# Hybrid decoder layer, prompt and one decode token: the channel parameters loaded by GpSimd's queue in two halves and turned in the gates' first step, two sums of gate rows on GpSimd, the decode gates' product in another bank

## The chip, the cores and the metric

The kernel runs on one core of a Trainium2 chip. The metric is the device time of one execution in microseconds (us). Before the change the median of three runs is 956.1 us (955.97 to 957.79).

## The reference

One decoder layer with two groups of heads is computed for a prompt of 1024 tokens and for one token each of 8 running sequences, all in float32. Cut to what matters here:

```python
hn = rmsnorm(x, g_norm)
u = hn @ w_in                       # 1024 -> 7 * 1024 + 4 + 4
xa, za, uq, uk, uv, uo, zb, ui, uf = jnp.split(u, SPLIT_IDX, axis=-1)
yA, hA, bufA = rglru_branch(xa, conv0, h0, conv_w, conv_b, w_rgate, b_rgate, w_igate, b_igate, lru_lambda)
...
ig = ui + b_mi                      # input gate, 4 heads
lf = jax.nn.log_sigmoid(uf + b_mf)  # forget gate, 4 heads
hB, C, n, m = mlstm_seq(q, k, v, ig, lf, C0, n0, m0)
yB = jax.nn.sigmoid(uo) * hB ; yB = headwise_rmsnorm(yB) * g_mhead
merged = jnp.concatenate([yA * jax.nn.silu(za), yB * jax.nn.silu(zb)], axis=-1)
x = x + merged @ w_out
```

`rglru_branch` needs parameters for each of its 1024 channels: `conv_w` (4 values), `conv_b`, `b_rgate`, `b_igate`, `lru_lambda`. `mlstm_seq` needs, for each token and head, sums and running maxima of the two gates over time, which come from `lf` and `ig`: 4 heads by 1024 tokens.

## The kernel before

**How the work is tiled.** TensorE multiplies a float32 pair as three products of parts (`mm3`, lines 62 to 66: high by high, high by low, low by high). The parts are made by `split` (lines 68 to 71): ScalarE casts the high part, VectorE subtracts it for the low part (`cb_hi`, `cb_lo` of the input; `wh`, `wl` of the weights). `w_in` is worked in 14 units (`UNITS`, line 44), each of two blocks of 256 columns, named by what they make: `v0v1` is unit 0, `x0y0` unit 1, `q0k0` unit 2.

**A unit.** From unit 1 on a unit is made by seven products in place of eight (a Strassen-like scheme; they come in the order P1, P2, P5, P6, P7, P3, P4, and "the third product" is P5). Each is 24 matmuls of 128x512 in two parts of 12, in a bank of PSUM with the tag `kv` (two banks; P1, P6, P7, P4) or `o` (three banks; P2, P5, P3). `evac` (line 300) takes a part out of its bank: ScalarE copies some (`s`, `c`), VectorE adds others (lines 316 and beside it), and `emit_out` (line 337) stores the result by GpSimd's queue (`stq`; `d_x`, `d_y`, `d_v` are the places in DRAM). Loads go by SyncE's queue (`ld`). `prep` (line 254) makes the weights' parts two products ahead, in a ring of six buffers (`ws`); at the third product it first calls `dec_unit`.

**Decode.** `dec_unit(u)` (line 227) multiplies the 8 decode tokens `hnd` by a unit's weights: eight matmuls of 32x512 (line 232) into the one bank with the tag `tr`, a copy `Z`, and later four transposes of it (line 240) into the same bank.

**The prelude** (lines 470 to 521). Nine tiles of x are fetched, scaled by the norm on VectorE, transposed (line 390) and split. Between them unit 0 is multiplied plainly (`plain`), 264 columns wide, since the 8 columns of the gates' weights `wg` go along; `gs` holds the prompt's gates as columns. After the loop the decode tokens' gates are multiplied (`pgd`, lines 512 to 514, in the `tr` bank), biased (`gd`, line 516), and stored to DRAM by SyncE's queue. Then `dec_unit(0)` and the loads of unit 1's weights (`load_raw`) follow.

**The gates** (`gates`, line 529) are a generator. Its steps stand in a list (`bg`), and in unit 1 two of them are popped after each part of a product, later one. In order:

- The 49 rows of parameters `par` (9 sources) are loaded by SyncE's queue; GpSimd fills `msk` and `stk`; `dgb`, the decode gates on all partitions, is loaded.
- Eight transposes (line 549) turn `par` to columns, which one VectorE copy puts into `PT` (line 550).
- A chain of small steps makes the log-sigmoid of the forget gates and of `lru_lambda` together (`gx`, lines 553 to 579).
- Transposes turn `lf` and `gs` to rows of 4x1024 (line 588), which are copied into `rows` (line 589). Two scans on VectorE run over time (lines 593 and 594).
- `al` (line 597) and `br` (line 600) are differences of such rows, `gsm` holds a few values for each chunk (lines 604 to 607).
- `stk` gathers four blocks of four rows: two sums on VectorE (lines 612 and 614), two copies on ScalarE.
- After five empty steps its eight transposes follow (line 622), and copies and exponentials of them (lines 624 to 627).

**What sets the order.** The kernel is written in one order of calls; a scheduler orders the instructions of each engine and places the waits. Each engine then works through its own list in order, and so does each queue of DMAs.

The functions that the diff touches, with the line numbers of the profile:

Of the kernel before, what the change touches and what calls it, by code (L numbers as in the profile page):

```python
# [9 lines left out]
F32 = mybir.dt.float32  # L10
# [3 lines left out]
ALU = mybir.AluOpType  # L14
# [3 lines left out]
P = 128  # L18
T = 1024
HT = 512  # L20
NB = 8
KC = 8
NH = 4
NCH = 8
L = 128
# [4 lines left out]
R_CW, R_CB, R_BR, R_BI, R_LAM, R_GM, R_H0, R_CONV, R_N0, R_END = 0, 4, 5, 6, 7, 8, 9, 17, 41, 49  # L30
# [19 lines left out]
def hymba_kernel(  # L50
# [28 lines left out]
    def ps(tag, shape):  # L79
        return psp.tile(shape, F32, tag=tag, name=f"ps_{tag}", bufs=NBUF.get(tag, 1))  # L80

    def const(shape, name, dt=F32):
        return cpool.tile(shape, dt, tag=name, name=name)
# [10 lines left out]
    def ws(shape, name, dt=F32R):  # L94

        return wsp.tile(shape, dt, tag="ws", name=name)

    def sg(shape, name, dt=F32):

        return stg.tile(shape, dt, tag="stg", name=name)  # L100
# [4 lines left out]
    def dconst(shape, name):  # L105

        return dpool.tile(shape, F32, tag=name, name=name)


    idF = const([P, P], "idF")  # L110
# [7 lines left out]
    PT = dconst([P, KC, R_END], "PT")  # L118
    bgate = const([P, 8], "bgate")
    m0b = dconst([P, NB, NH], "m0b")  # L120
# [33 lines left out]
    d_gd = dram.tile([NB, 8], F32, name="d_gd")  # L154
# [72 lines left out]
    def dec_unit(u):  # L227

        pz = ps("tr", [P, 512])
        for k in range(KC):  # L230
            g = k % 4
            TE.matmul(pz[32 * g:32 * g + 32, :], hnd[:, NB * k:NB * k + 32], raws[u, k // 4][:, k % 4, :], start=k < 4, stop=k >= 4,  # L232
                      skip_group_check=True)
        Z = sg([P, 512], "Z")
        A.copy(Z, pz)

        def turn():
            pt = ps("tr", [P, 4, P])
            for m in range(4):
                TE.transpose(pt[:, m, :], Z[:, m * P:(m + 1) * P], idF)  # L240
            for a, (kind, j) in enumerate(units[u]):
                src = pt[:, 2 * a:2 * a + 2].rearrange("p m (g b) -> p m b g", g=4)[:, :, 0:NB, :]
                V.tensor_reduce(dec_dst[kind](j), src, axis=mybir.AxisListType.X, op=ALU.add)
                if kind == "k":
                    V.tensor_scalar(dec_dst[kind](j), dec_dst[kind](j), 1.0 / 16.0, None, op0=ALU.mult)
        late.append(turn)
# [115 lines left out]
    fp = es_f.enter_context(tc.tile_pool(name="f_start", bufs=1))  # L362
# [85 lines left out]
    def plain(i):  # L448
# [10 lines left out]
        for w in range(2):  # L459
# [7 lines left out]
                V.tensor_tensor(gs[:, i, :], pt[:, 256:264], bgate, op=ALU.add)  # L467
            stq(d_v[w][i * P:(i + 1) * P, :], t)

    pw = ps("tr", [P, P])  # L470

    for _ in range(17):
# [36 lines left out]
            plain(i)  # L509
            x_combos(i)  # L510

    pgd = ps("tr", [32, 8])
    for k in range(KC):
        TE.matmul(pgd, hnd[:, NB * k:NB * k + 32], wg[:, k, :], start=k == 0, stop=k == KC - 1)
    gd = dconst([NB, 8], "gd")
    V.tensor_tensor(gd, pgd[0:NB], bgate[0:NB], op=ALU.add)
    ld(d_gd, gd)
    dec_unit(0)
    load_raw(1, 0)
    load_raw(1, 1)  # L520
# [4 lines left out]
    fp = es_f.enter_context(tc.tile_pool(name="f_gates", bufs=1, reuse_waits="tile"))  # L525
# [1 line left out]
    LOHI = slice(0, 64), slice(64, 128)  # L527

    def gates():

        par = ws([R_END, T], "par", F32)
        ld(par[R_CW:R_CW + 4, :], conv_w[0])
        for r, t in ((R_CB, conv_b), (R_BR, b_rgate), (R_BI, b_igate), (R_LAM, lru_lambda), (R_GM, g_mhead)):
            ld(par[r:r + 1, :], t)
        ld(par[R_H0:R_H0 + NB, :], st_h[0])
        ld(par[R_CONV:R_CONV + 24, :], st_conv[0].rearrange("b j w -> (b j) w"))
        ld(par[R_N0:R_N0 + NB, :], st_n[0].rearrange("b h k -> b (h k)"))
        ld(m0b, st_m[0].partition_broadcast(P))
        stk = fp.tile([P, T], F32, tag="stk", name="stk")
        msk = fp.tile([NH, T], F32, tag="msk", name="msk")  # L540
        G.memset(msk, 1.0)
        G.memset(msk.rearrange("p (c l) -> p c l", l=L)[:, :, 0:1], 0.0)
        G.memset(stk, 0.0)
        dgb = fp.tile([P, NB, 8], F32, tag="dgb", name="dgb")
        ld(dgb, d_gd.partition_broadcast(P))
        yield
        pt = ps("s", [P, KC, 64])
        for j in range(KC):
            TE.transpose(pt[:, j, 0:R_END], par[:, j * P:(j + 1) * P], idF[:R_END, :R_END])
        V.tensor_copy(PT, pt[:, :, 0:R_END])  # L550
        yield

        gx = fp.tile([P, 6, 72], F32, tag="gx", name="gx")
        fx, ab, lg, z, z2, p = (gx[:, n, :] for n in range(6))
# [37 lines left out]
        mr, br = rows1[:, 0, :], rows1[:, 1, :]  # L592
# [3 lines left out]
        al = lfr  # L596
# [4 lines left out]
        c3 = lambda t: t.rearrange("p (c l) -> p c l", l=L)  # L601
        sm = fp.tile([NH, 3, NCH], F32, tag="gsm", name="gsm")
        mpv, aL, csr = sm[:, 0], sm[:, 1], sm[:, 2]
# [5 lines left out]
        ld(d_cs, csr)  # L609
        ld(cs_b, d_cs.partition_broadcast(P))  # L610
        yield
        V.tensor_tensor(c3(stk[0:4]), c3(al), mpv.unsqueeze(2).to_broadcast([NH, NCH, L]), op=ALU.add)
        A.copy(stk[32:36], br)
        V.tensor_tensor(c3(stk[64:68]), c3(br), aL.unsqueeze(2).to_broadcast([NH, NCH, L]), op=ALU.add)
        A.mul(stk[96:100], mr, -1.0)
        for _ in range(5):
            yield
        for half in range(2):
# [4 lines left out]
            s = slice(half * 4, half * 4 + 4)  # L623
# [10 lines left out]
    bg, rgq, dcq = deque(), deque(), deque()  # L634
# [740 lines left out]
    def preps(n):  # L1375
        while state["prep"] < min(n, len(seq)):
            prep(*seq[state["prep"]])
            state["prep"] += 1

    gg = gates()  # L1380
    bg.extend([lambda: next(gg, None)] * 17 + [rd_open])
    last_u = len(units) - 1
    unit_of = {p: u for u, pair in enumerate(units) for p in pair}
    done_h = [max(unit_of[k, h] for k in "qkv") for h in range(NH)]
# [60 lines left out]
    for n in range(4, N):  # L1445
        c, h = n // 4, n % 4
# [90 lines left out]
```

## Time and profile before

| what | value |
|---|---|
| median of three runs | 956.1 us (955.97 to 957.79) |
| the profiled execution, its own time | 955.33 us |
| its span in the profile | 953.5 us |
| its mean granted TensorE clock | 0.995 |
| TensorE (PE) busy | 929.5 us, 97% |
| VectorE (DVE) busy | 713.0 us, 75% |
| ScalarE (ACT) busy | 584.7 us, 61% |
| GpSimd (POOL) busy | 146.2 us, 15% |

Times in the rows of a timeline are microseconds from the start of the span. A row gives the start, the duration, the engine, the line of the code, the operation, and what it writes and reads (`out<-in`, the program's names with the buffer numbers left out, so that `ps_s` is the bank with the tag `s`). In square brackets stands how long the engine was idle just before, and what ended that. A row of waits gives the sum, the count and the longest. SPq and POOLq are the queues of DMAs that SyncE and GpSimd issue.

### The profile page before, as it was taken

To read this page: it belongs to the slowest core of one execution; us is meant where nothing else is said; L and a number is where in the kernel's file an instruction comes from. 1 tells how busy PE (TensorE), PEld (TensorE's weight loads), DVE (VectorE), ACT (ScalarE), POOL (GpSimd) and SP (SyncE) were. 2 spreads that over 40 slices of the span, in tenths; PEclk is the share of its full clock that TensorE was granted. 3 is DMA by queue.
4 is the path that set the end of the run, shared out by engine and by line. 5 is a ranking of instruction groups with operands and counts; after the bars stand their busy time and mean duration, and the time that the engine had idled before them with its cause. 6 is when DMAs were issued, how large, how long until landed. Compare 5 with 4: busy or idle time off the path is not lost.

```text
span 953.5 us, 15405 instructions
## 1 busy us (share of the span) xinstructions
PE 929.5 (97%) x5370; PEld 763.6 (80%) x5370; DVE 713.0 (75%) x1482; ACT 584.7 (61%) x1046; POOL 146.2 (15%) x259
## 2 busy tenths in 40 slices
PE   7999999999999999999999999999999999999997
PEld 7887767777787987776789998876567888888886
DVE  5876798879798877988887867686566677676754
ACT  5664347778677757677677774465546466555532
POOL 1111112112212122111122221010200100000020
PEclk9999999999999999999999999999999999999999
DMA  5441447355745465445647362534863654564361
GB/s 185 148 128 40 136 119 266 109 183 194 259 142 206 156 206 171 166 155 171 223 153 244 122 219 84 161 111 146 297 213 95 204 162 119 162 179 143 111 110 51
DMA packets 131363, 153.71 MB, mean 161 GB/s; under 512 B 15798, under 2 KB 110038, under 8 KB 131278
## 3 DMA queue, kind: packets, MB, share of 16 engines
q1 hardware_dynamic: 113558, 96.86, 34.1%
q0 software_dynamic: 17728, 55.87, 16.2%
q8 instruction: 42, 0.69, 0.3%
q14 instruction: 35, 0.29, 0.1%
HBM read 101.11 MB, written 51.65 MB: 160 GB/s over the span
## 4 chain that ended last, share of the span: by engine, by line
PE 75%; DVE 9%; DMA 7%; issue 4%; ACT 3%; SPq 1%; POOL 0%; DVEq 0%; ACTq 0%; POOLq 0%
PE ps_o L64 12%; PE ps_o L66 12%; PE ps_o L65 12%; PE ps_kv L64 9%; PE ps_kv L66 9%; PE ps_kv L65 9%; DMA W<-d_alpha 3%; PE ps_tr L232 2%; PE ps_s L1087 1%; DVE wl L71 1%; PE ps_qp L914 1%; DMA x<-in_x_prompt_dram 1%; PE ps_tr L1223 1%; PE ps_s L747 1%; PE ps_qp L64 1%
## 5 line engine op out<-in xcount | busy, mean ns | idle before, releaser
L70 ACT CAST wh<-raw 128x1024 fp32r<-128x1024 f32 x91 | 95.6, 1051 | 58.5 <-PE ps_o L65 22.7
L71 DVE TENSOR_TENSOR wl<-raw,wh 128x1024 fp32r<-128x1024 f32 x91 | 111.2, 1222 | 26.8 <-ACT wh L70 16.3
L64 PE MATMUL ps_kv<-cb_hi,wh 128*128 128x512 f32 x320 | 128.1, 400 | 0.4 <-ACT s L313 0.4
L66 PE MATMUL ps_kv<-cb_hi,wl 128*128 128x512 f32 x320 | 125.7, 393 | 0.0
L65 PE MATMUL ps_kv<-cb_lo,wh 128*128 128x512 f32 x320 | 125.1, 391 | 0.0
L64 PE MATMUL ps_o<-cb_hi,wh 128*128 128x512 f32 x240 | 95.0, 396 | 0.0
L66 PE MATMUL ps_o<-cb_hi,wl 128*128 128x512 f32 x240 | 94.1, 392 | 0.0
L65 PE MATMUL ps_o<-cb_lo,wh 128*128 128x512 f32 x240 | 93.4, 389 | 0.0
L64 PEld LDWEIGHTS ps_kv<-cb_hi,wh 128*128 128x128 f32 x320 | 60.1, 188 | 23.5 <-issue 5.5
L66 PEld LDWEIGHTS ps_kv<-cb_hi,wl 128*128 128x128 f32 x320 | 60.1, 188 | 15.6 <-issue 2.5
L65 PEld LDWEIGHTS ps_kv<-cb_lo,wh 128*128 128x128 f32 x320 | 60.2, 188 | 12.6 <-issue 0.8
L64 PE MATMUL ps_kv<-wh,cb_hi 128*128 128x256 f32 x192 | 55.4, 288 | 0.0
L65 PE MATMUL ps_kv<-wl,cb_hi 128*128 128x256 f32 x192 | 54.3, 283 | 0.0
L66 PE MATMUL ps_kv<-wh,cb_lo 128*128 128x256 f32 x192 | 54.3, 283 | 0.0
L64 PE MATMUL ps_o<-wo,rh 128*128 128x512 f32 (+1 forms) x136 | 53.8, 396 | 0.0
L64 PEld LDWEIGHTS ps_o<-cb_hi,wh 128*128 128x128 f32 x240 | 45.1, 188 | 10.7 <-issue 1.8
L66 PEld LDWEIGHTS ps_o<-cb_hi,wl 128*128 128x128 f32 x240 | 45.0, 188 | 10.6 <-issue 0.8
L64 PE MATMUL ps_o<-wo,mh 128*128 128x512 f32 (+1 forms) x136 | 52.8, 388 | 0.0
L66 PE MATMUL ps_o<-wo,ml 128*128 128x512 f32 (+1 forms) x136 | 51.9, 382 | 0.6 <-DVE ml L71 0.6
L65 PEld LDWEIGHTS ps_o<-cb_lo,wh 128*128 128x128 f32 x240 | 45.1, 188 | 9.2
L66 PE MATMUL ps_o<-wo,rl 128*128 128x512 f32 (+1 forms) x136 | 51.9, 382 | 0.3 <-DMA rl<-d_rm 0.3
L65 PE MATMUL ps_o<-wo,rh 128*128 128x512 f32 (+1 forms) x136 | 51.8, 381 | 0.0
(475 smaller groups left out, 2541.9 us busy)
## 6 DMA issues: line engine op xcount, KB each, us to landing
raw<-in_w_in_dram SPq DMA_DIRECT2D x56, 512.0 KB
Cb<-in_state_mlstm_C_dram SPq DMA_DIRECT2D x32, 256.0 KB
out_dram<-Cb POOLq DMA_DIRECT2D x32, 256.0 KB, 4.7
qk<-d_qk SPq DMA_DIRECT2D x32, 256.0 KB
oraw<-in_w_out_dram SPq DMA_DIRECT2D x16, 512.0 KB
d_qk<-s POOLq DMA_DIRECT2D x24, 256.0 KB, 3.8
x<-in_x_prompt_dram SPq DMA_DIRECT2D x8, 512.0 KB
d_x<-s POOLq DMA_DIRECT2D x16, 256.0 KB, 2.6
```

Source lines behind the costliest of these rows:

```text
L64: TE.matmul(out, ah, bh, start=first, stop=False, skip_group_check=True)
L65: TE.matmul(out, ah, bl, start=False, stop=False, skip_group_check=True)
L66: TE.matmul(out, al, bh, start=False, stop=last, skip_group_check=True)
L70: A.copy(hi, src)
L71: V.tensor_tensor(lo, src, hi.bitcast(F32), op=ALU.subtract)
L232: TE.matmul(pz[32 * g:32 * g + 32, :], hnd[:, NB * k:NB * k + 32], raws[u, k // 4][:, k % 4, :], start=k < 4, stop=k >= 4, skip_group_chec ...
L747: TE.matmul(pg, w[:, n, :], st["xx"][n], start=k == 0, stop=k == 1)
L914: TE.matmul(pq[32 * g:32 * g + n, 0:256], q, ds_["C", h * NB + bb][:, kb, :], start=b == 1, stop=b == NB - 1, skip_group_check=True)
L1087: TE.matmul(S, qk[:, 2 + kb, :], qk[:, kb, :], start=kb == 0, stop=kb == 1)
L1223: TE.matmul(dec_o[0][32 * g:32 * g + 32, :], md, oraw[m][:, half * 512:(half + 1) * 512], start=n == 0, stop=n == 14, skip_group_check=True)
```

## The change

Lines of the changed kernel are named here by their new numbers.

- `par_load(half)` (new) loads the nine sources of the parameters for 512 channels each into a staging tile, by GpSimd's queue. Both halves are loaded in the prelude, ahead of `dec_unit(0)`; `m0b` and `dgb` too, and the store of `gd` goes to the same queue, ahead of the load of `dgb`.
- The decode gates' product `pgd` stands in a bank with the tag `o`, where it stood in the `tr` bank.
- The gates' first step turns the two halves, four transposes each, and ScalarE copies each half to `PT`. The steps of loading and turning are one now, so that 16 steps are popped where there were 17.
- The two sums into `stk` are GpSimd's.

```diff
+    def par_load(half):
+
+        hs = slice(half * HT, (half + 1) * HT)
+        par = sg([R_END, HT], f"par{half}")
+        stq(par[R_CW:R_CW + 4, :], conv_w[0][:, hs])
+        for r, t in ((R_CB, conv_b), (R_BR, b_rgate), (R_BI, b_igate), (R_LAM, lru_lambda), (R_GM, g_mhead)):
+            stq(par[r:r + 1, :], t[:, hs])
+        stq(par[R_H0:R_H0 + NB, :], st_h[0][:, hs])
+        stq(par[R_CONV:R_CONV + 24, :], st_conv[0].rearrange("b j w -> (b j) w")[:, hs])
+        stq(par[R_N0:R_N0 + NB, :], st_n[0].rearrange("b h k -> b (h k)")[:, hs])
+        pars.append(par)
...
-    pgd = ps("tr", [32, 8])
+    pgd = ps("o", [32, 8])
...
-    ld(d_gd, gd)
+    stq(d_gd, gd)
+    dgb = dconst([P, NB, 8], "dgb")
+    stq(dgb, d_gd.partition_broadcast(P))
+    stq(m0b, st_m[0].partition_broadcast(P))
+    for half in range(2):
+        par_load(half)
     dec_unit(0)
...
     def gates():
-
-        par = ws([R_END, T], "par", F32)
-        ld(par[R_CW:R_CW + 4, :], conv_w[0])
...
-        ld(m0b, st_m[0].partition_broadcast(P))
+        for half in range(2):
+            pt = ps("s", [P, 4, 64])
+            for j in range(4):
+                TE.transpose(pt[:, j, 0:R_END], pars[half][:, j * P:(j + 1) * P], idF[:R_END, :R_END])
+            A.copy(PT[:, 4 * half:4 * half + 4], pt[:, :, 0:R_END])
+        yield
...
-        dgb = fp.tile([P, NB, 8], F32, tag="dgb", name="dgb")
-        ld(dgb, d_gd.partition_broadcast(P))
-        yield
-        pt = ps("s", [P, KC, 64])
-        for j in range(KC):
-            TE.transpose(pt[:, j, 0:R_END], par[:, j * P:(j + 1) * P], idF[:R_END, :R_END])
-        V.tensor_copy(PT, pt[:, :, 0:R_END])
-        yield
...
-        V.tensor_tensor(c3(stk[0:4]), c3(al), mpv.unsqueeze(2).to_broadcast([NH, NCH, L]), op=ALU.add)
+        G.tensor_tensor(c3(stk[0:4]), c3(al), mpv.unsqueeze(2).to_broadcast([NH, NCH, L]), op=ALU.add)
         A.copy(stk[32:36], br)
-        V.tensor_tensor(c3(stk[64:68]), c3(br), aL.unsqueeze(2).to_broadcast([NH, NCH, L]), op=ALU.add)
+        G.tensor_tensor(c3(stk[64:68]), c3(br), aL.unsqueeze(2).to_broadcast([NH, NCH, L]), op=ALU.add)
...
-    bg.extend([lambda: next(gg, None)] * 17 + [rd_open])
+    bg.extend([lambda: next(gg, None)] * 16 + [rd_open])
```

The change moves instructions on every engine. On GpSimd, at the end of the prelude, the last stores of unit 0 (`d_v`) and the fills of `msk` and `stk` stood before like this:

```order
L468 DMA d_v_130<-pe 128x256
L468 DMA d_v_131<-pe 128x256
L541 MEMSET msk 4x1024
L543 MEMSET stk 128x1024
L542 MEMSET msk 4x8
```

Now the same place reads, up to the last but one load of the first half (`par_1009`):

```order
L530 DMA d_gd<-gd 8x8
L474 DMA par_1009<-in_conv_w_dram 4x512
L468 DMA d_v_130<-pe 128x256
L476 DMA par_1009<-in_conv_b_dram 1x16x32
L532 DMA dgb<-d_gd 128x64
L476 DMA par_1009<-in_b_rgate_dram 1x16x32
L468 DMA d_v_131<-pe 128x256
L476 DMA par_1009<-in_b_igate_dram 1x16x32
L476 DMA par_1009<-in_lru_lambda_dram 1x16x32
L476 DMA par_1009<-in_g_mhead_dram 1x16x32
L477 DMA par_1009<-in_state_rglru_h_dram 8x512
L478 DMA par_1009<-in_state_rglru_conv_dram 24x512
```

Loads of the parameters stand between and behind the two stores; the second half's nine follow, and the fills come after them.

On TensorE, the transposes of `stk` (L622) stood before in the first product of unit 2, whose matmuls are those that read `cb_hi_156` and `cb_lo_157`:

```order
L240 MATMUL ps_tr<-idF,Z 128x128 x4
L64 MATMUL ps_kv<-cb_hi_156,wh_0_1394 128x512
L65 MATMUL ps_kv<-cb_lo_157,wh_0_1394 128x512
L66 MATMUL ps_kv<-cb_hi_156,wl_0_1395 128x512
L64 MATMUL ps_kv<-cb_hi_156,wh_0_1394 128x512
L65 MATMUL ps_kv<-cb_lo_157,wh_0_1394 128x512
L622 MATMUL ps_s<-idF,stk 128x128 x4
L622 MATMUL ps_qp<-idF,stk 128x128 x4
L66 MATMUL ps_kv<-cb_hi_156,wl_0_1395 128x512
```

Now they (L629) stand in the sixth product of unit 1 (P3, reading `cb_hi_166`), after 15 of its 24 matmuls:

```order
L64 MATMUL ps_o<-cb_hi_166,wh_5_1298 128x512
L65 MATMUL ps_o<-cb_lo_167,wh_5_1298 128x512
L66 MATMUL ps_o<-cb_hi_166,wl_5_1299 128x512
L629 MATMUL ps_s<-idF,stk 128x128 x4
L629 MATMUL ps_qp<-idF,stk 128x128 x4
L64 MATMUL ps_o<-cb_hi_166,wh_5_1298 128x512
```

The rest of the sixth product and the whole seventh, which stood ahead of them, stand behind them.

On VectorE, the second half of the gates' chain, from the scans to the two sums, read before:

```order
L593 SCALAR_TENSOR_TENSOR rows_1206<-rows_1160 4x1024
L594 SCALAR_TENSOR_TENSOR rows_1206<-msk,rows_1160 4x1024
L605 COPY gsm<-rows_1206 4x7
L335 SCALAR_TENSOR_TENSOR c_1442<-tz,c_1442 128x512
L597 TENSOR_TENSOR rows_1160<-rows_1206 4x1024
L257 TENSOR_TENSOR raw_2_1244<-raw_2_1244 128x4x256
L600 TENSOR_TENSOR rows_1206<-rows_1160,rows_1206 4x1024
L606 COPY gsm<-rows_1160 4x8
L612 TENSOR_TENSOR stk<-rows_1160,gsm 4x1024
L607 TENSOR_TENSOR gsm<-gsm 4x8
L614 TENSOR_TENSOR stk<-rows_1206,gsm 4x1024
```

Now, with the weights' part `wl_6` of the seventh product ahead of it:

```order
L596 COPY rows_1172<-ps_s 4x512 x2
L71 TENSOR_TENSOR wl_6_1343<-raw_1_1043,wh_6_1342 128x1024
L600 SCALAR_TENSOR_TENSOR rows_1218<-rows_1172 4x1024
L601 SCALAR_TENSOR_TENSOR rows_1218<-msk,rows_1172 4x1024
L612 COPY gsm<-rows_1218 4x7
L316 TENSOR_TENSOR s_1272<-s_1272,ps_kv 128x512
L604 TENSOR_TENSOR rows_1172<-rows_1218 4x1024
L335 SCALAR_TENSOR_TENSOR s_1272<-tz,s_1272 128x512
L607 TENSOR_TENSOR rows_1218<-rows_1172,rows_1218 4x1024
L613 COPY gsm<-rows_1172 4x8
```

The two sums are gone from here; they stand on GpSimd, with one store of `d_y` (line 343) between them.

More of the change, by code (lines that the diff above doesn't have):

```diff
@@ L468, in plain @@
             stq(d_v[w][i * P:(i + 1) * P, :], t)
+    def par_load(half):
[8 more added lines that the diff above has]
+        pars.append(par)
+    pars = []
     pw = ps("tr", [P, P])
@@ L529, in gates @@
     def gates():
-        par = ws([R_END, T], "par", F32)
[L532 to L537, printed above, removed]
-        ld(m0b, st_m[0].partition_broadcast(P))
+        for half in range(2):
[4 more added lines that the diff above has]
+        yield
         stk = fp.tile([P, T], F32, tag="stk", name="stk")
```

## The prediction

> **What bounds the kernel now.** I read the page first, then the busy times in stretches of ten microseconds, then TensorE's own waits, then the timeline of each engine around them.
>
> ```profile
> span 953.5 us, 15405 instructions
> ...
> PE 929.5 (97%) x5370; PEld 763.6 (80%) x5370; DVE 713.0 (75%) x1482; ACT 584.7 (61%) x1046; POOL 146.2 (15%) x259
> ```
>
> TensorE is busy for 97% of the span, so only two things can move the end: TensorE's work, which the change leaves at the same instructions, and TensorE's waits. The order of all five engines is the old one again from about 155 us on, so the whole effect is made before that.
>
> ```profile
> core 0: us, PE busy (x) PEld busy (x) DVE busy (x) ACT busy (x) POOL busy (x), PEclk, DMA share, GB/s
> ...
> 40.00:50.00 10.00, 10.00 (x82) 8.24 (x75) 8.70 (x18) 6.07 (x14) 1.29 (x3) 1.00 0.69 214
> ...
> 110.00:120.00 10.00, 9.73 (x47) 7.51 (x46) 9.79 (x25) 3.27 (x7) 2.17 (x4) 1.00 0.38 138
> 120.00:130.00 10.00, 8.33 (x48) 5.26 (x47) 9.94 (x13) 4.60 (x7) 1.10 (x2) 1.00 0.08 29
> ...
> 140.00:150.00 10.00, 8.38 (x37) 6.60 (x36) 7.41 (x14) 6.30 (x10) 2.01 (x3) 1.00 1.00 297
> ```
>
> From 110 to 130 us VectorE (DVE) is full, and TensorE loses 1.7 us in the second of these stretches and 1.6 in the one from 140. TensorE's waits from 60 to 150 us, with what ended them, are these four:
>
> ```profile
> PE ps_s L622 <- DVE stk L614: 1.7, 1, 1.7
> PE ps_s L747 <- DVE xh L741: 1.6, 1, 1.6
> PE ps_o L66 <- DVE cb_lo L71: 1.1, 2, 0.8
> PE ps_s L588 <- DVE gx L560: 0.3, 1, 0.3
> ```
>
> L622 and L588 belong to the gates' chain, which the change moves; 1.7 + 1.6 + 0.3 us are what it can win there.
>
> **The start of the program.**
>
> ```profile
> 29.45 0.80 PE L514 MATMUL ps_tr<-wg,hnd 128*32 128x8 f32 x16 [0.48 <-DVE hnd L398]
> 30.95 0.63 PE L390 MATMUL ps_s<-idF,x 128*128 128x128 f32 x4 [0.70 <-DVE gd L516]
> ...
> 71.66 0.39 PE L66 MATMUL ps_o<-wph,cb_lo 128*128 128x264 f32 x1 [0.83 <-DVE cb_lo L71]
> ...
> 77.15 1.92 PE L232 MATMUL ps_tr<-raw,hnd 128*32 128x512 f32 x16
> ```
>
> The gates' decode product (0.80) stood in a hole that lasts anyway until VectorE has scaled the next x tile, so removing it there wins nothing. It comes back near 71 us, in the 0.83 hole of L66: cost nothing, since VectorE's `cb_lo` covers it, and 0.8 if that cover is gone. The eight products of decode unit 0 cost 1.92 / 8 = 0.24 each; five now fill the hole at 29.45, three stand two groups later, and seven leave later places. That wins 7 x 0.24 = 1.7 at most, if none of those places was a hole.
>
> ```profile
> 35.67 1.06 ACT L375 ACTIVATE junk<-x 128x1024 bf16<-128x1024 f32 x1 [0.73 <-DMA x<-in_x_prompt_dram]
> ...
> 40.91 0.93 SPq L219 DMA_DIRECT2D raw<-in_w_in_dram  x2
> ```
>
> Against it: with the `tr` bank free earlier, weight unit 1's first megabyte is asked for at about 31 us, ahead of an x tile, where it was asked for at 40.91. ScalarE already waits 0.73 for that tile, and a megabyte at the 214 GB/s of that stretch is 4.9 us, while the tile is multiplied only some 10 us later. I take 1.1 us of the win as lost to this: **-0.6**, between -1.7 (all won) and +1.0 (the wait returns behind ScalarE, without a win).
>
> **The parameters on GpSimd's queue.**
>
> ```profile
> 75.34 0.54 POOL L468 DMA_DIRECT2D d_v<-pe  x1 [5.18 <-ACT pe L465]
> 77.97 0.54 POOL L468 DMA_DIRECT2D d_v<-pe  x1 [2.08 <-ACT pe L465]
> ...
> 79.39 0.95 POOL L543 MEMSET stk<- 128x1024 f32 x1
> ```
>
> ```profile
> 85.61 0.27 SPq L532 DMA_DIRECT2D par<-in_conv_w_dram  x1
> ```
>
> ```profile
> d_v<-pe POOLq DMA_DIRECT2D x16, 128.0 KB, 2.4
> ```
>
> SyncE loses 12 issues like this one, of about 0.3 us, for which nobody waited; GpSimd gets 21, of which `m0b` stands at the start. Five stand before the `d_v` store of 77.97, in idle time; fifteen follow from 78.5: 15 x 0.54 = 8.1. The first half's last parameter (the sixth) starts at 81.2 and, with the 2.4 of a store from issue to landing, is there at 83.6; the second half's starts at 86.1 and is there at 88.5. TensorE asks for the halves after these products, at the pitch of these rows:
>
> ```profile
> 144.09 0.39 PE L64 MATMUL ps_kv<-cb_hi,wh 128*128 128x512 f32 x1
> 144.31 0.39 PE L65 MATMUL ps_kv<-cb_lo,wh 128*128 128x512 f32 x1
> ```
>
> A wide product takes 0.23 from start to start. Decode unit 1's group has left 77.15, so unit 1 begins there: 28 products (6.4), four row transposes (0.4), decode unit 1 (1.9) to the first half at 85.9; 22 more products and 16 small transposes (1.3) to the second at 92.2. So 2.3 and 3.7 us are to spare, and the loads cost **nothing**; the cover is gone at 0.54 + 2.3/6 = 0.92 us per issue for the first half, and 0.54 + 3.7/15 = 0.79 for the second. `dgb` now starts near 76.4 and lands near 79; VectorE comes to it at about 78.1, and behind it wait the two subtractions for the third product, which has until 91 us: nothing. PT's copy goes from VectorE to ScalarE in two parts beside other work.
>
> **The chain and its end.**
>
> ```profile
> 104.08 0.17 DVE L557 COPY gx<-PT 128x8 f32<-128x8 f32 x1
> ...
> 110.44 1.22 DVE L71 TENSOR_TENSOR wl<-raw,wh 128x1024 fp32r<-128x1024 f32 x1
> ...
> 111.72 0.69 DVE L335 SCALAR_TENSOR_TENSOR s<-tz,s 128x512 f32<-128x512 f32 x1
> ...
> 114.12 0.23 DVE L560 SCALAR_TENSOR_TENSOR gx<-gx 128x72 f32<-128x72 f32 x1
> ...
> 118.23 2.28 DVE L593 TENSOR_TENSOR_SCAN rows<-rows 4x1024 f32<-4x1024 f32 x1
> 120.44 2.25 DVE L594 TENSOR_TENSOR_SCAN rows<-msk,rows 4x1024 f32<-4x1024 f32 x1
> ...
> 128.07 1.22 DVE L614 TENSOR_TENSOR stk<-rows,gsm 4x1024 f32<-4x1024 f32 x1
> ```
>
> ```profile
> 114.50 0.60 PE L588 MATMUL ps_s<-idF,gx 128*4 128x128 f32 x4 [0.27 <-DVE gx L560]
> ...
> 129.44 0.63 PE L622 MATMUL ps_s<-idF,stk 128*128 128x128 f32 x4 [1.67 <-DVE stk L614]
> ```
>
> PT is whole near 93.1 and VectorE free for it at 93.4, after the last weight subtraction. L557 to L560's start took 10.0 with two `wl` (1.13 each, start to next), five adds of 512 (0.6 each), and two more decode products; now it is three `wl` and one add: 10.0 + 1.1 - 2.4 = 8.7, so L560 starts at 102.1 and L588, 0.38 behind it as before, at 102.5. TensorE is there after 40 products (9.1) and the second half (0.4), at 101.8: it waits **0.7**.
>
> The second group of row transposes now has five products ahead of it, so its copy ends at 105.2. Next in VectorE's order is the seventh product's `wl`, whose weights wait for a buffer that TensorE gives up near 104.8: cast 1.05, subtraction 1.1, so the scans start at 107.1 and take 4.4. With one add and `al` (1.2) behind them, `al` is there at 113.4. GpSimd starts 0.29 after what it waits for, by the scan's end (118.23 + 2.28) and this store:
>
> ```profile
> 120.80 0.53 POOL L599 DMA_DIRECT2D out_dram<-rows  x1 [3.48 <-DVE rows L593]
> ```
>
> No row shows an add on GpSimd. These bound it:
>
> ```profile
> 0.24 0.10 POOL L1523 MEMSET const-float32-0.0<- 128x1 f32 x1 [0.24 <-issue]
> ...
> 1.36 0.20 POOL L115 MEMSET maskT<- 128x128 f32 x1
> ...
> 1.75 0.28 POOL L116 TENSOR_SCALAR_AFFINE_SELECT maskT<-maskT 128x128 f32<-128x128 f32 x1
> ```
>
> Below it is the fill of 1024 columns, 0.95. A column written costs (0.95 - 0.20) / 896 = 0.84 ns, and one read besides (0.28 - 0.20) / 128 = 0.63 ns; two reads and a write are 2.1 ns, 2.15 us for 1024 columns and 0.10 to start. Above, the whole select's 2.2 ns a column and half as much again for the second read, 3.4. I take 2.3, since the select is the nearest row. The Trainium skill, page "GPSIMD Engine Reference", section "3.1 Elementwise — side-by-side cycle accounting", measured 4497 ns for such an add of 2048 columns; half of it, as an estimate, would leave the sum as it is, and no run here shows it yet.
>
> Then: first add 113.7 to 116.0; a `d_y` store stands between (0.54) until 116.6; second add until 118.9; transposes at 119.0. TensorE, after L588, has 45 products (10.3) and 0.9 of transposes: it is there at 113.7 and waits **5.3** where it waited 1.67. Behind it stand the rest of the sixth product and all of the seventh, and VectorE's `be_t`. With VectorE relieved of 2.4 us of adds and TensorE some 5 us later, the conv's casts are ready long before L747, which also stands after 25 us of TensorE work from L622, not 15: its 1.6 goes.
>
> Sum: 0.7 - 0.3 + 5.3 - 1.7 - 1.6 - 0.6 = **+1.8**. The profiled execution took 955.33 by itself; the three runs' median is 956.1, 0.8 above. On the median's scale: **957.9**.
>
> **Rivals.** *GpSimd adds at VectorE's price* (1.2, as L614): both adds save 2.2, the wait is 3.1, and the sum is -0.4: 955.7; with all of the start's 1.7, 954.6. It decides below an add of 1.4 us. For it: four rows are little data, and the fill's 0.84 ns. Against: the select's row.
>
> *The adds and VectorE shut each other out.* The first add is ready while VectorE runs L335, with L600 (1.2, two inputs in SBUF) next. Should the two engines' SBUF reads exclude each other, one waits for the other, and the second add needs both: 1.2 later, 959.1. Nothing in this trace shows GpSimd reading beside VectorE. The Trainium skill, page "SBUF — State Buffer", section "SBUF: two separate sides", says that they share a port pair as an exclusive lock between a VectorE instruction with two SBUF inputs and a GpSimd instruction that reads SBUF; by that rule this rival is the forecast.
>
> *The parameters come late.* If a narrow load costs GpSimd 1.0 us, the second half is 15 x 0.46 - 3.7 = 3.2 late, TensorE waits at its transposes, and all behind moves: 961.1. Against it: the widest issues of GpSimd take 0.72,
>
> ```profile
> L897 POOL DMA_DIRECT2D out_dram<-Cb x32 | 23.0, 718 | 66.4 <-DVE Cb L895 13.1 <-ACT s L353 11.4 <-ACT wh L70 9.1
> ```
>
> with VectorE busy nearly all of the time.
>
> **Numbers.** Forecast 0.45, cheap adds 0.27, shut-out 0.15, late loads 0.13. About 0.2% (1.9 us) is what a measurement of this kernel can tell from no change. The forecast, 957.9 give or take 1.5, lies half beyond 958.0: slower 0.22, same 0.23; cheap adds: faster 0.14, same 0.13; the two others are slower. Faster 0.14, same 0.36, slower 0.50. Range: 953.5 (an add of 0.95 and all of the start's win) to 962.5 (late loads and an add of 3.4 share the top).
>
> **What would show it.** Right: a TensorE wait of 4 to 7 us at the `stk` transposes near 113 us, released by GpSimd; none at L747; `par` transposes without a wait; GpSimd adds near 2.3. Wrong: a wait at the `par` transposes, adds near 1.2, or TensorE beginning unit 1 outside 75.5 to 78.2. If VectorE's order holds it up elsewhere than at the seventh `wl`, the 5.3 is wrong.

## The result, and the profile after

The changed kernel takes 963.13 us in the median of six runs (962.46 to 965.17), where the kernel before takes 956.65 (955.97 to 957.79). The ratio is 1.0071, with a 95% interval from 1.0055 to 1.0087: it is slower, by 6.5 us. The forecast was 957.9, the range ended at 962.5. The profiled execution took 962.86 us.

The page of the changed kernel:

```profile
span 961.1 us, 15414 instructions
...
PE 932.7 (97%) x5370; PEld 766.8 (80%) x5370; DVE 712.4 (74%) x1479; ACT 583.6 (61%) x1048; POOL 160.3 (17%) x282
```

TensorE has the same 5370 matmuls, yet 3.2 us more of busy time: some of them ran slower. Its waits from 76 to 200 us, of the changed kernel:

```profile
PE ps_s L629 <- POOL stk L621: 4.6, 1, 4.6
PE ps_s L754 <- DVE xh L748: 0.3, 1, 0.3
PE ps_s L595 <- DVE gx L567: 0.3, 1, 0.3
```

The wait for `stk` stands there as forecast, released by GpSimd, and the 1.6 us at the conv's products (L747 before, L754 now) have shrunk to 0.3. The `par` transposes (L551) do not appear, and their rows carry no wait either:

```profile
86.83 0.45 PE L551 MATMUL ps_s<-idF,par 49*128 49x49 f32 x4
...
93.33 0.45 PE L551 MATMUL ps_s<-idF,par 49*128 49x49 f32 x4
```

What the list of waits cannot show is the speed behind the wait. This is TensorE's own timeline of the changed kernel there, in the sixth product and the first row of the seventh (`ps_kv`):

```profile
114.26 0.39 PE L66 MATMUL ps_o<-cb_hi,wl 128*128 128x512 f32 x1
119.21 1.11 PE L629 MATMUL ps_s<-idF,stk 128*128 128x128 f32 x4 [4.56 <-POOL stk L621]
...
120.83 0.78 PE L64 MATMUL ps_o<-cb_hi,wh 128*128 128x512 f32 x1
...
124.64 0.40 PE L64 MATMUL ps_kv<-cb_hi,wh 128*128 128x512 f32 x1
```

Nine matmuls take 3.81 us from 120.83 to 124.64, 0.42 from start to start, where 0.23 is usual. The table by stretches of the changed kernel has the reason in the column PEclk (after the busy times of the five engines):

```profile
114.19:117.60 3.41, 0.45 (x3) 0.03 (x1) 3.41 (x4) 0.48 (x1) 2.71 (x3) 1.00 0.17 60
117.60:121.01 3.41, 1.80 (x9) 1.81 (x10) 3.36 (x5) 1.63 (x6) 1.55 (x1) 0.50 0.07 26
121.01:124.43 3.42, 3.42 (x10) 2.65 (x10) 1.51 (x9) 0.34 (x3) 1.43 (x5) 0.50 0.48 164
124.43:127.84 3.41, 3.41 (x16) 2.80 (x15) 1.91 (x2) 1.29 (x2) 0.54 (x1) 1.00 0.92 209
```

The granted clock falls to half at 117.60, while TensorE is still waiting, and stays there until 124.43. In the kernel before, no stretch between 110 and 150 us had less than 1.00. By the Trainium skill, page "TensorE: Matmul & The Clock Gate", section "HAM oscillation — how this bites in real kernels", idle gaps above about 3.4 us bring the clock to half. The trace agrees for this gap of 4.7 us; shorter ones are told of below.

GpSimd's sums and VectorE beside them, in the changed kernel:

```profile
113.80 2.21 POOL L619 TENSOR_TENSOR stk<-rows,gsm 4x1024 f32<-4x1024 f32 x1 [3.31 <-DVE rows L604]
...
117.27 1.89 POOL L621 TENSOR_TENSOR stk<-rows,gsm 4x1024 f32<-4x1024 f32 x1 [0.70 <-DVE gsm L613]
```

```profile
114.19 2.90 DVE L607 TENSOR_TENSOR rows<-rows,rows 4x1024 f32<-4x1024 f32 x1
...
117.10 0.67 DVE L316 TENSOR_TENSOR s<-s,ps_kv 128x512 f32<-128x512 f32 x1
117.69 1.48 DVE L614 TENSOR_TENSOR gsm<-gsm 4x8 f32<-4x8 f32 x1
```

The sums take 2.21 and 1.89, near the 2.3 of the forecast. VectorE's subtraction L607, 1.2 us by itself, takes 2.90: it ends 1.1 after the first sum does, as if it had begun only then. The same shows at L614, which adds 32 numbers in 1.48 us beside the second sum, whereas L316, with one input in PSUM, keeps its 0.67 beside it.

### The profile page after: what moved, and what is told of

It is laid out like the page before. It is cut to its first block, busy times and chain, and to the rows that moved or that the text cites. A ratio compares the mean times of both kernels' runs of the same rounds, so it can differ in the third digit from the quotient of the medians.

```text
span 961.1 us, 15414 instructions
## 1 busy us (share of the span) xinstructions
PE 932.7 (97%) x5370; PEld 766.8 (80%) x5370; DVE 712.4 (74%) x1479; ACT 583.6 (61%) x1048; POOL 160.3 (17%) x282
## 4 chain that ended last, share of the span: by engine, by line
PE 78%; DVE 9%; DMA 7%; ACT 3%; issue 2%; POOL 0%; SPq 0%; ACTq 0%; DVEq 0%; POOLq 0%
PE ps_o L66 12%; PE ps_o L64 12%; PE ps_o L65 12%; PE ps_kv L64 9%; PE ps_kv L65 9%; PE ps_kv L66 9%; PE ps_tr L232 3%; DMA oraw<-in_w_out_dram 2%; DMA x<-in_x_prompt_dram 1%; PE ps_s L1094 1%; DVE wl L71 1%; DMA W<-d_alpha 1%; PE ps_qp L921 1%; PE ps_qp L64 1%; PE ps_qp L65 1%
## 5 line engine op out<-in xcount | busy, mean ns | idle before, releaser
L66 PE MATMUL ps_kv<-cb_hi,wl 128*128 128x512 f32 x320 | 125.5, 392 | 0.0
```

Of the source, the lines that this page charges most:

```text
L66: TE.matmul(out, al, bh, start=False, stop=last, skip_group_check=True)
```

## The experiments

Theory A: the early loss is the wait for GpSimd's sums, which the shut-out of VectorE lengthens, and the half clock behind it. Theory B: it is the parameters' loads on GpSimd's queue or the bank, in the prelude. Theories L1 and L2 are on the part of the loss that comes after 655 us. Every ratio is to the kernel before on the same chip.

### 1 and 2: both kernels, unchanged, a second time

> The kernel before, unchanged, profiled a second time. The change's profile lies 7.5 us above that of before: 4.3 of it is there at 200 us, the other 3.3 comes after 690 us, where both kernels run the same instructions in the same order. Theory L1 (the late part is chance: when the output weights' transfer lands): this profile's TensorE wait near 697 us is another than the 2.2 us of the first (anything from 1 to 4), and its span differs by 1 us or more from 953.5. Theory L2 (the late part is a steady echo of the change): the wait is 2.2 again, give or take 0.3, and the span 953.5 give or take 0.7.

> The changed kernel, unchanged, profiled a second time. The stk transposes: the same wait of 4.6 us, GpSimd's adds 2.2 and 1.9, VectorE's subtraction beside the first add at 2.9 in place of 1.2, granted clock 0.50 for about 7 us behind the wait. Late part: by L1 a wait that differs from 3.6 us by over 0.5; by L2 3.6 again, with half clock from 701 to 708.

The same instruction in each (VectorE's weight subtraction, in unit 1, unit 4 and unit 13) serves as a mark in time. The kernel before, first profile and second:

```profile
69.78 1.23 DVE L71 TENSOR_TENSOR wl<-raw,wh 128x1024 fp32r<-128x1024 f32 x1 [1.92 <-PE ps_kv L390]
...
203.36 1.22 DVE L71 TENSOR_TENSOR wl<-raw,wh 128x1024 fp32r<-128x1024 f32 x1
...
655.50 1.23 DVE L71 TENSOR_TENSOR wl<-raw,wh 128x1024 fp32r<-128x1024 f32 x1 [1.02 <-ACT wh L70]
```

```profile
span 958.9 us, 15405 instructions
...
68.14 1.23 DVE L71 TENSOR_TENSOR wl<-raw,wh 128x1024 fp32r<-128x1024 f32 x1 [1.93 <-PE ps_kv L390]
...
202.17 1.22 DVE L71 TENSOR_TENSOR wl<-raw,wh 128x1024 fp32r<-128x1024 f32 x1
...
653.82 1.23 DVE L71 TENSOR_TENSOR wl<-raw,wh 128x1024 fp32r<-128x1024 f32 x1 [0.63 <-ACT wh L70]
```

The changed kernel, first profile:

```profile
70.78 1.23 DVE L71 TENSOR_TENSOR wl<-raw,wh 128x1024 fp32r<-128x1024 f32 x1 [2.56 <-PE ps_kv L390]
...
207.60 1.22 DVE L71 TENSOR_TENSOR wl<-raw,wh 128x1024 fp32r<-128x1024 f32 x1
...
659.12 1.23 DVE L71 TENSOR_TENSOR wl<-raw,wh 128x1024 fp32r<-128x1024 f32 x1 [0.53 <-ACT wh L70]
```

The mark of unit 4 in its second profile:

```profile
208.44 1.22 DVE L71 TENSOR_TENSOR wl<-raw,wh 128x1024 fp32r<-128x1024 f32 x1
```

From the last mark to the end of the span the kernel before takes 953.5 - 655.5 = 298.0 in one execution and 958.9 - 653.8 = 305.1 in the other. The changed one takes 302.0, and 299.7 in its second profile. So the late part swings by 7 us in one and the same kernel, and the 4.0 us by which the first pair differed there cannot be put down to the change. A part of the swing is one wait near 697 us, for ScalarE's work behind the output weights' transfer. It is here in the waits of before, first profile and second:

```profile
PE ps_qp L64 <- ACT hh L1143: 2.2, 1, 2.2
```

```profile
PE ps_qp L64 <- ACT hh L1143: 3.6, 1, 3.6
```

In the changed kernel's two profiles it is 3.6 and 4.1, with half clock behind it for 7 us in the one and 3.4 in the other. L1 holds and L2 falls. The early part repeats: the changed kernel's second profile has the same wait of 4.6 for `stk` and the same half clock, from 118.6 to 125.5. What the change costs stands ahead of 200 us: 207.60 and 208.44 against 203.36 and 202.17, 4.2 to 6.3 us by the pair that is taken.

### 3: both sums back on VectorE

```diff
-        G.tensor_tensor(c3(stk[0:4]), c3(al), ...)
+        V.tensor_tensor(c3(stk[0:4]), c3(al), ...)
-        G.tensor_tensor(c3(stk[64:68]), c3(br), ...)
+        V.tensor_tensor(c3(stk[64:68]), c3(br), ...)
```

> The changed kernel with both sums back on VectorE. Theory A (the early loss is the wait for GpSimd's sums, lengthened by the shut-out of VectorE, and the half clock that follows): the subtraction ahead of the sums takes 1.2 again, stk is whole near 118.0, TensorE comes to its transposes 1.4 us later by its order (6 products), so the wait falls from 4.6 to about 2.2; if 2.2 is short enough for the full clock, 5 us in all are won (958.1), if the clock is still halved for some 3 us, 3.5 (959.6). Theory B (the loss is in the parameters' loads and the prelude): within 1.5 us of the changed kernel, 962 to 964.

Measured: 958.75, ratio 1.0026 (1.0011 to 1.0041), 4.4 us less than the changed kernel. Its rows on VectorE and on TensorE:

```profile
114.32 1.20 DVE L607 TENSOR_TENSOR rows<-rows,rows 4x1024 f32<-4x1024 f32 x1
```

```profile
118.21 0.63 PE L629 MATMUL ps_s<-idF,stk 128*128 128x128 f32 x4 [2.06 <-DVE stk L621]
...
119.03 0.48 PE L64 MATMUL ps_o<-cb_hi,wh 128*128 128x512 f32 x1
```

The subtraction takes 1.20 at the same place, the wait is 2.06, and the clock stays at 1.00. The eight transposes take 0.82 (118.21 to 119.03), where they took 1.62 at half clock; with the nine matmuls behind them (3.81 for 9 x 0.23 = 2.07) the half clock cost the changed kernel 0.80 + 1.74 = 2.5 us. Theory A's first figure was 958.1; B would have stayed near 963.

### 4, 7 and 8: the bank of the decode gates' product

```diff
-    pgd = ps("o", [32, 8])
+    pgd = ps("tr", [32, 8])
```

> The changed kernel with the decode gates' product in the tr bank again. Theory A: unit 1's first product begins 0.5 to 1.5 us earlier than the 78.06 of the changed kernel, since the x tile is no longer behind the next weights' megabyte (TensorE's wait of 1.05 at 41 us gone), but the chain of the gates is not earlier, so that the wait for stk grows by as much and the time stays within 1 us of 963.1. Theory B (the prelude is what is lost): 1 to 2 us faster, 961 to 962.

> The kernel before with nothing but the decode gates' product in an o bank. If the bank's move is what makes the prelude later (unit 1's weights asked for at 31 us, the x tile 2.8 us later, TensorE waiting 1 us for its cast): unit 1's first product some 0.9 us later than 79.0, all else as before, time 0 to 1.5 us above before. If the prelude's shift comes from the parameters on GpSimd's queue instead: unit 1 at 79.0 or earlier, time equal or up to 1.7 lower.

> The changed kernel with both sums on VectorE and the decode gates' product in the tr bank: what is left of the change is the parameters' loads and the turning in the first step. Theory A: no half clock before 690 us, a wait for stk of 1.5 to 2.5, unit 1 about 1 us earlier than with the o bank; 956.5 to 959, within 2 us of before and not above the 958.75 of the kernel with the sums alone put back by more than 1. Theory B (the parameters are the loss): 960 or more.

Run 4 makes this edit in the changed kernel, run 7 the opposite one in the kernel before, run 8 this edit together with that of run 3. Run 4: 961.86 (1.0056, 1.0037 to 1.0075), which is the time that B gave, though its interval overlaps that of the changed kernel; the wait for `stk` did not grow by what the start won, as A had it, but is 4.3, with half clock behind it. Run 7: 957.72 (1.0013, 0.9996 to 1.0030), which cannot be told from no change. Each of the two puts the bank at some 1.4 us, and neither can be told from nothing. Unit 1 begins at 77.08 in run 4, 1.0 earlier than in the changed kernel, as theory A had it; in run 7 it begins at 78.40, between the 79.00 and the 77.37 of the two profiles of the kernel before. The x tile does come late wherever the product stands in the `o` bank: ScalarE waits 1.43 for it in the changed kernel and 1.40 in run 7, where it waits 0.73 in the kernel before. But the start of the program differs by 1.6 us between two profiles of the kernel before (69.78 and 68.14 above), so that a microsecond there needs more runs than these. Run 8 missed: 962.52 (1.0074, 1.0060 to 1.0088), where 956.5 to 959 was expected and B said 960 or more. Yet what it shows is no wait for a parameter. Its two longest waits from 76 to 200 us:

```profile
PE ps_tr L232 <- ACT ig L704: 2.8, 1, 2.8
PE ps_s L629 <- DVE stk L621: 1.9, 1, 1.9
```

A new wait of 2.8 has come at 173 us: the decode group of a later unit wants the `tr` bank, which the conv's gates hold until ScalarE has read them (`ig`); run 4 has the same wait, of 1.1. The order that the scheduler made of this program brought the two together. Each of the two waits has half clock behind it, for 3.4 us. So a kernel with none of GpSimd's sums can be as slow as the changed one, through another wait of the same kind.

### 5: the sums alone, in the kernel before

```diff
-        V.tensor_tensor(c3(stk[0:4]), c3(al), ...)
+        G.tensor_tensor(c3(stk[0:4]), c3(al), ...)
-        V.tensor_tensor(c3(stk[64:68]), c3(br), ...)
+        G.tensor_tensor(c3(stk[64:68]), c3(br), ...)
```

> The kernel before with nothing but the two sums moved to GpSimd. Theory A (sums on GpSimd lengthen the chain whose end TensorE waits for: 2.2 and 1.9 in place of 1.2 each, and a VectorE instruction with two inputs in SBUF stands still beside them): the transposes of stk stand 5 products' worth earlier in TensorE's order, stk is whole about 0.5 to 1.5 us later than its 129.3, so the wait grows from 1.7 to 3 or more and half clock follows: 2 to 5 us slower than before. Theory A' (the loss came only from the transposes' new place, sixth product of unit 1): the wait grows by under 1 us, no half clock, time within 1.5 us of before.

Measured: 961.92, ratio 1.0068 (1.0051 to 1.0085): this edit by itself costs 5.7 us. The sums, VectorE's subtraction (L600 in this kernel) and TensorE's wait, in run 5:

```profile
124.61 2.74 POOL L612 TENSOR_TENSOR stk<-rows,gsm 4x1024 f32<-4x1024 f32 x1 [0.43 <-DVE rows L597]
128.59 3.49 POOL L614 TENSOR_TENSOR stk<-rows,gsm 4x1024 f32<-4x1024 f32 x1 [1.24 <-DVE gsm L606]
```

```profile
125.53 2.90 DVE L600 TENSOR_TENSOR rows<-rows,rows 4x1024 f32<-4x1024 f32 x1
...
129.11 1.21 DVE L258 TENSOR_TENSOR raw<-raw,raw 128x1024 f32<-128x1024 f32 x1
```

```profile
PE ps_s L622 <- POOL stk L614: 5.9, 1, 5.9
```

Here it goes both ways: the subtraction stands still for the first sum, and the second sum takes 3.49 in place of 1.89 while VectorE's L258, with both inputs in SBUF, keeps its 1.21. The wait is 5.9, and half clock follows from 131.6 to 135.0. Theory A holds in kind (3 or more and half clock), though its 2 to 5 us were too few; A' falls: the sums cost as much at the old place of the transposes.

### 11: only the second sum on GpSimd

```diff
-        G.tensor_tensor(c3(stk[0:4]), c3(al), ...)
+        V.tensor_tensor(c3(stk[0:4]), c3(al), ...)
```

> The changed kernel with the first sum on VectorE and only the second on GpSimd. Theory A: the subtraction ahead of the sums takes 1.2 again, since no sum runs beside it; the second sum begins near 115.8 beside VectorE's first sum, which has two inputs in SBUF, and one of the two stands still for the other: stk whole at 118.3 to 119, the wait 3.5 to 4.5, half clock again; 961 to 963.5, that is, nearly all of the loss with one sum. If the two engines do not exclude each other: stk whole at 117.8, the wait 3.0 to 3.3.

Measured: 960.48, ratio 1.0045 (1.0025 to 1.0064), below the 961 to 963.5 of theory A. The sum and VectorE, then TensorE's wait:

```profile
116.21 2.73 POOL L621 TENSOR_TENSOR stk<-rows,gsm 4x1024 f32<-4x1024 f32 x1 [0.49 <-DVE gsm L613]
```

```profile
114.76 1.21 DVE L607 TENSOR_TENSOR rows<-rows,rows 4x1024 f32<-4x1024 f32 x1
...
115.97 1.21 DVE L619 TENSOR_TENSOR stk<-rows,gsm 4x1024 f32<-4x1024 f32 x1
117.11 1.85 DVE L614 TENSOR_TENSOR gsm<-gsm 4x8 f32<-4x8 f32 x1
```

```profile
PE ps_s L629 <- DVE gsm L614: 3.5, 1, 3.5
```

With no sum beside it L607 takes 1.21; beside VectorE's own sum GpSimd's takes 2.73, 0.84 more than the 1.89, and then L614 stands still for it. (The wait is put down to L614, since it ends at 118.96, just behind the sum's 118.94.) The wait is 3.5, with one stretch of half clock. The mechanism is as expected, the time lies between the kernels with none and with two.

### 6 and 10: dummy products in the wait

```diff
+        pw2 = ps("s", [P, 512])
+        for n in range(5):
+            TE.matmul(pw2, al[:, 0:P], al[:, 0:512], start=True, stop=True)
         for half in range(2):
             pk = ps(("s", "qp")[half], [P, 4, P])
```

> The changed kernel with five dummy products more (4 partitions, 512 columns, float32, of the row al by itself, their result unused) ahead of the stk transposes, which the scheduler then puts 12 products earlier. They can begin when al is there (113.7) and take some 4 us, so that TensorE's one idle stretch of 4.7 becomes two of 2 us and 1 us; stk is whole at the same 119.2. Theory C (half clock is the echo of an idle stretch longer than about 2.2 us): granted clock 1.00 from 112 to 130, the 12 products that now stand behind cost 2.7 more and the clock gives back 2.6: 962 to 964. Theory D (half clock comes from the sums or the transposes, not from idling): 0.50 again for 7 us, 965.5 or more.

> As the run with dummy products of 4 partitions, which did not keep the clock, but the five dummies read a tile of 128 partitions (ones, with a few values of al copied in, so that they can begin at about 114.4). They stand 9 products earlier than the changed kernel's transposes. Theory C' (the clock gate counts the work of the array, and 4 of 128 rows are as good as idle): idle is 2 us and below 1 us with full-height products between, granted clock 1.00 from 112 to 130, the five take about 4.5 us, 962 to 964.5. Theory D (the drop comes from the sums or from what follows, whatever TensorE does): 0.50 again for some 7 us, 965 or more.

Run 6: 965.85 (1.0109, 1.0095 to 1.0123). Run 10: 965.37 (1.0098, 1.0070 to 1.0126). Neither kept the clock, and both times are those of theory D. In run 10 the test was spoiled: the copy that frees the dummies stood still beside GpSimd's first sum (1.86 for 4x32), and TensorE idled for 3.7 us before them. What the two tell stands in how the half clock ends. Run 6, with products of 4 rows from 113.93 to 121.7 and full-height work from there, then run 10, with full-height products from 117.59 on:

```profile
115.00:118.50 3.50, 3.50 (x6) 1.40 (x5) 3.50 (x4) 1.04 (x1) 2.80 (x3) 0.50 0.19 75
118.50:121.90 3.40, 3.40 (x5) 0.85 (x4) 2.54 (x3) 0.73 (x2) 1.35 (x2) 0.50 0.01 1
121.90:125.30 3.40, 3.40 (x13) 3.01 (x13) 1.09 (x8) 0.67 (x6) 0.35 (x4) 0.51 0.25 88
125.30:128.70 3.40, 3.40 (x17) 2.78 (x16) 0.84 (x2) 0.41 (x1) 0.54 (x1) 1.00 0.42 115
```

```profile
119.60:123.00 3.40, 3.40 (x6) 1.33 (x5) 2.79 (x3) 0.77 (x3) 1.35 (x2) 0.50 0.00 0
123.00:126.40 3.40, 3.40 (x16) 2.05 (x15) 0.59 (x5) 0.54 (x6) 0.56 (x4) 0.97 0.22 82
```

In run 10 one stretch of 3.4 us filled with full-height products ended the half clock. In run 6 TensorE was busy without a gap through two such stretches, with products that use 4 of the 128 rows, and the clock stayed at half; it came back after the first stretch of full-height work. So 4-row products count as idle here: theory C', for the end of the half clock. D, by which the sums or the transposes make it and not the idling, falls by runs 8 and 12, where half clock follows waits at other products with no sum on GpSimd. That full-height products in the wait would have prevented the fall was not shown.

### 9: the parameters on SyncE's queue

```diff
-        stq(par[R_CW:R_CW + 4, :], conv_w[0][:, hs])
+        ld(par[R_CW:R_CW + 4, :], conv_w[0][:, hs])
```

All nine loads of `par_load` go so, and both sums are VectorE's.

> The changed kernel with both sums on VectorE and the parameters' loads on SyncE's queue; the bank o is kept. Against the kernel with the sums alone put back (958.75) only the queue of these loads differs, and with it the order: the first half is turned 8 rows and the stk transposes 11 rows earlier in TensorE's list. If the loads on GpSimd's queue cost nothing (as forecast): 957 to 961, the wait for stk 2 to 4.5 since TensorE comes some 2.5 us earlier to it, with half clock if over about 2.2. If they do cost: 955 to 957, faster than before.

Measured: 961.33, ratio 1.0047 (1.0029 to 1.0065), above the 957 to 961 of the one case and far from the 955 to 957 of the other. The wait for `stk` is 1.6, where 2 to 4.5 was expected, and keeps the full clock, but the wait of 2.8 at L232 has come as in run 8, with half clock behind it. So the time says nothing on the queue by itself: what was to be one difference brought another. That the loads on GpSimd's queue cost TensorE nothing rests on the rows of the changed kernel, whose `par` transposes do not wait.

### 12: the first sum on ScalarE, in the kernel before

```diff
-        V.tensor_tensor(c3(stk[0:4]), c3(al), ...)
+        for c in range(NCH):
+            A.activation(c3(stk[0:4])[:, c, :], c3(al)[:, c, :], AF.Identity, bias=mpv[:, c:c + 1])
```

> The kernel before with the first sum moved to ScalarE, as eight activations of 4x128 with the chunk's value as bias; the second stays on VectorE, GpSimd has none. Theory A (GpSimd was the wrong helper, because of its speed and the shut-out; another engine can take the sum): the eight take about 0.2 to 0.25 each, 1.6 to 2 in all, beside VectorE, whose subtraction keeps its 1.2; stk is whole up to 1.2 us earlier than 129.3, the wait falls from 1.7 to between 0.2 and 1.2, the clock stays full there: 954.5 to 956.5, a little faster than before or not to be told from it. Against it: the eight stand ahead of ScalarE's copy of br and of casts, and if ScalarE is late with these the wait is as long as before or longer, 956.5 to 959.

Measured: 958.35, ratio 1.0018 (1.0005 to 1.0031), no gain; it lies in the 956.5 to 959 of the case against theory A. ScalarE takes the sum without touching VectorE, whose subtraction keeps 1.21, but the eight take 2.45, where 1.6 to 2 was expected, and the waits move on:

```profile
125.90 2.45 ACT L613 ACTIVATE stk<-rows,gsm 4x128 f32<-4x128 f32 x8 [1.65 <-DVE rows L597]
```

```profile
PE ps_s L748 <- DVE xh L742: 3.0, 2, 2.6
PE ps_s L623 <- ACT Z L235: 1.8, 1, 1.8
```

The wait ahead of the `stk` transposes is 1.8, as long as before. The profile puts it down to ScalarE's copy of the decode group, which ends at 130.12; VectorE's second sum ends at 130.08, so that either may have held the transposes. The wait at the conv's products has grown to 2.6, with half clock. No version here beats the kernel before.

## Why the prediction was wrong

| step of the sum, us | forecast | profile pair |
|---|---|---|
| start of the program | -0.6 | +1.0 |
| row transposes (L588, now L595) | +0.4 | 0.0 |
| wait for `stk` | 5.3 - 1.7 = +3.6 | 4.6 - 1.7 = +2.9 |
| conv's products (L747, now L754) | -1.6 | -1.3 |
| half clock behind the wait | 0 | +2.5 |
| sum | +1.8 | +5.1 |
| seen at 203 to 208 us | | +4.2 |

Of the 0.9 between the last two rows, 0.4 is a second, shorter wait at the conv's products: L747 waits 2.0 in two pieces before, L754 0.3 in one. The rest is not put down to a place. The second profile of the changed kernel has the same waits (4.6, 0.4 and 0.3) and as long a half clock.

**The step that failed** is the one under "The chain and its end": "it is there at 113.7 and waits **5.3** where it waited 1.67". It priced a wait by its length alone. The wait came, with the releaser and nearly the length that were forecast, but it is followed by half clock, which the waits of 1.7 and 1.6 of the kernel before did not have behind them. That term of 2.5 us was missing from the sum and from every rival, so that no case reached 963. Run 3, which takes GpSimd out, wins 4.4 us; run 5, which puts GpSimd alone in, loses 5.7. The signs that the prediction named as right came (a wait of 4 to 7 us released by GpSimd, no wait at the `par` transposes, sums near 2.3, unit 1 at 78.06; only at the conv's products 0.3 is left where none was named), so the chain itself was read rightly. A second term, the start, was mis-sized by 1.6 in the first pair.

**The shut-out** had 0.15 as a rival, at 1.2 us. It is shown: 2.90 beside a sum, 1.20 without one. By the Trainium skill, page "SBUF — State Buffer", section "SBUF: two separate sides", the two engines hold a shared port pair as an exclusive lock; the traces agree, in both directions. It did not lengthen the forecast's wait, because other errors ran against it: the second sum took 1.89 in place of 2.3, and TensorE came at 114.5 in place of 113.7.

**GpSimd's sums**: 2.3 forecast, 2.21 and 1.89 measured when VectorE is not in the way. The rival of cheap sums falls. **The parameters**: no wait at their transposes, as forecast; the last load begins at 86.41, forecast 86.1. **The seventh `wl`, the scans, `al`**: forecast 107.1 for the scans and 113.4 for `al`, measured 107.41 and 113.66.

**The start** was forecast at -0.6 with an end at +1.0 for the case that the x tile comes late; in the first pair it came late and cost 1.0. Unit 1 begins at 78.06, 0.94 before the 79.00 of the kernel before, but without a decode group of 1.92, which now stands later. Since the same kernel's start differs by 1.6 between two profiles, the size stays open.

**The scale.** The forecast added its sum to one profiled execution, whose late part, 298.0, was the shortest of the four. The kernel before's median was 956.65 beside the changed kernel and 956.3 to 957.2 in later runs, so that the 0.8 allowed for that was 0.1 to 1.0 too little. The low end of the range does not follow from its own terms: sums of 0.95 save 2.7 and the start's win 1.1 more, which makes 954.1 and not 953.5.

What stays open: the 2.4 us by which run 3 is above the kernel before (1.0011 to 1.0041). It has the late x tile, a wait for `stk` of 2.1 and a new one of 1.2 for ScalarE's copy of a decode group; runs 8 and 9, which differ from it by one edit each, meet another wait instead. By its profile most of this stands in the start: unit 1 begins at 78.20 with the decode group of 1.92 still to come, 1.1 and 2.8 later than in the two profiles of before, and from there to the mark of unit 4 (204.94) it takes, less that group, 124.8 against their 124.4 and 124.8. But that is one profile of a start that swings by 1.6, and no run separates the x tile from the rest of the prelude.

## What to carry to other kernels

In this kernel a wait of TensorE costs its length only while it is short: ask of each wait of 2 us or more what the clock does behind it, and add that to the sum. Work that is given to GpSimd to relieve VectorE can relieve nothing if VectorE's next instruction reads two inputs from SBUF, since the one then stands still for the other: here two sums of 1.2 left VectorE, and L607 and L614 took 1.7 and 1.3 longer beside them. Look at what runs beside such work, not only at how long it takes. And where the late part of a program swings by several microseconds from run to run, compare two profiles by marks within the program before reading a difference of spans.

## What the runs showed of the hardware

- Half clock comes in stretches of 3.4 us and multiples: behind 100 us in fourteen traces, both kernels and all runs, it lasted about 3.4, 7 or 10 us (the last stretch, which runs into the program's end, left out), and the clock lost over a stretch, (1 - granted) x time, came to 1.7, 3.4 or 5.1 us. In each trace all changes of the clock lie whole multiples of 3.413 us apart, to within 0.002 us; in the changed kernel those at 15.20, 117.60, 124.43, 701.28 and 708.11, for example. So a grid of windows of 3.413 us runs through each execution, and it lies otherwise in each one.
- Behind 100 us, with idle time counted from start to start of two products less 0.23, no idle stretch of TensorE below 2.1 us was followed by half clock (run 6 left out, where 4-row products follow one of 2.0), and every one of 3.1 us or more was. Between these, eight were (2.10, 2.38, 2.76, 2.80, 2.95, 2.96, 2.99, 3.00) and four were not (2.22, 2.23, 2.88, 3.02). So the length alone does not decide there, and the 3.4 us of the Trainium skill (page "TensorE: Matmul & The Clock Gate", section "HAM oscillation — how this bites in real kernels") is too long as a limit for this kernel.
- What decides is how much of the idle time falls into one window of the grid. With idle time as the profile has it, from the end of one product to the start of the next, all 23 falls behind 100 us (that of the last stretch again left out) stand at the end of a window with 1.77 us or more of it, and none of the other windows has more than 1.91. Half clock ended behind windows with at most 0.55 and went on behind those with 0.63 or more (run 6's 4-row products again left out). Run 3's wait of 2.06 kept the clock because it lay across two windows, 0.37 in the first and 1.69 in the second; run 8's of 1.95 lay in one and lost it:

```profile
116.52:119.93 3.41, 1.72 (x12) 1.62 (x13) 3.35 (x7) 1.04 (x4) 0.35 (x3) 1.00 0.04 7
```

```profile
114.12:117.53 3.41, 1.47 (x8) 0.96 (x7) 3.35 (x6) 2.25 (x4) 0.00 (x0) 1.00 0.80 238
117.53:120.94 3.41, 3.41 (x13) 3.03 (x12) 2.86 (x9) 1.15 (x7) 0.93 (x4) 0.50 0.28 92
```

- By these figures (an estimate, from 2 x 1.91) a wait of over 3.8 us, such as the changed kernel's 4.6, cannot miss the half clock, and one of 1.8 to 3.8 meets it or not by chance. The full clock of run 3's profile was in part such chance.
- The fall can come when TensorE is working again: in the first profile of the kernel before it idled from 695.2 to 697.6, and the clock was at half from 699.0 to 702.4.
- A VectorE instruction on 32 numbers (L614) takes 0.15 us in run 3 and 1.85 beside a GpSimd sum in run 11; a copy of 4x32 took 1.86 beside one in run 10.
